# The inverse of the 16x16 blocks in two RWKV layers: rows brought to all partitions through DRAM, one product and one sum a column

## The chip, the cores and the metric

One NeuronCore of a Trainium2 chip runs the whole program in one launch. The metric is the device time of an execution in microseconds. Before the change three runs gave a median of 3160.73 us (3151.62 to 3163.76).

## What is computed

Six layers over 256 tokens of width 2048, all in float32: RWKV-7, dilated attention, pooling, a second RWKV-7 layer, then an even and an odd layer of another family. The change lies in the two RWKV layers. Their core in the reference is a recurrence over the tokens, for 32 heads of 64 channels:

```python
def step(state, inp):
    r_t, w_t, k_t, v_t, a_t, b_t = inp
    sa = jnp.einsum('bhij,bhj->bhi', state, a_t)
    state = (state * w_t[:, :, None, :] + sa[..., None] * b_t[:, :, None, :]
             + v_t[..., None] * k_t[:, :, None, :])
    y_t = jnp.einsum('bhij,bhj->bhi', state, r_t)
    return state, y_t
```

The kernel does it in chunks of 64 tokens. Within a chunk the effect of the a and b terms on each other is the inverse of a 64x64 matrix (identity minus a strictly triangular one) for each head and chunk. That inverse is built up: 16x16 diagonal blocks first, by substitution column by column; from them 32x32 blocks and then the whole by matrix products.

## The kernel before

**Projections.** `proj` (L238 on) multiplies 256 tokens by 512 columns of a weight matrix. Each 256x512 piece of weights is a DMA from SP's queue into one of three tiles `wr` (L225). ACT casts it to a high part `wh` (L220), DVE subtracts to get the low part `wl` (L221), five tiles of each, and PE makes three products for each of two token halves and each 128 rows (L262): 12 instructions of 512 columns for one `wr`. An RWKV layer has sixteen such projections (for k, r, v and a gate, `a_w_in`) and an output projection `a_w_out`, done in two passes: inputs 0 to 1535 first (`st`, L387), the last 512, which come from the layer's last two blocks, after that.

**Blocks.** `rwkv_block` treats four heads at a time, 256 channels, so there are eight blocks to a layer. A block loads its k, v, r and small weights (`ld`, `vt`, `lw`), forms factors, and multiplies them into the chunks' matrices `GM` (L842 on PE, L845 on DVE). ACT copies the 16x16 diagonal parts to `Md` (L860), and ACT and DVE select from them `Mc` (L863, L864). `Mc` is [128, 16, 8]: its partition is 16 x (one of eight 16-row groups) + row, its free axes are the column c and one of 8 units u (a head and a pair of chunks), so all 64 diagonal blocks of four heads lie in one tile. `Xc` of the same form begins as the identity. The recurrence runs over r = 0 to 14: `stream_shuffle` brings row r of each 16-row group to all partitions of the group (L871), the later columns of that row are multiplied by column r of Xc (L876), and the products are added to the columns behind it, the next one apart (L879, L881). L932 then lays Xc out as the blocks of `X`; products on PE (L929, L956) complete the inverse. Last come the four chunks in sequence (L990, L998, L1008, L1022), where each needs the state of the one before, a normalisation of the result `yt` over DVE, POOL and ACT (L1036 to L1049), and `z` (L1055), which is transposed (L277) and split for the output projection.

**Order.** The order of the code is written by a small planner: the projections advance a clock (`pump`), and blocks are generators that say with `yield` after how many microseconds they go on. A block waits there for marks of other blocks: it copies `Md` only when the block before has set `rec`, that is when its recurrence is written. `urgent` marks the blocks' instructions with a higher priority. The framework then schedules every engine's instructions by its own model of time, and each engine runs its list in that order. SP issues all loads and stores, weights among them, in one list; an instruction of it that waits holds up what stands behind.

Of the kernel before, what the change touches and what calls it, by code (L numbers as in the profile page):

```python
# [11 lines left out]
F32 = mybir.dt.float32  # L12
FR = mybir.dt.float32r
I32 = mybir.dt.int32
AF = mybir.ActivationFunctionType
OP = mybir.AluOpType
AX = mybir.AxisListType
# [97 lines left out]
class Builder:  # L115
# [562 lines left out]
    def rwkv_block(self, ia, b):  # L678

        nc, I, S = self.nc, self.I, self.S  # L680
# [9 lines left out]
        def tmp():  # L690
            return self.t("e2", B2, F32, 7)
# [112 lines left out]
        pr = tmp()  # L804
# [50 lines left out]
        Md = self.t("Md", [128, 32, 8], F32, 1)  # L855
        for i in range(4):
            rs = slice(i * 32, i * 32 + 32)
            for f in range(2):
                us = slice(f * 4, f * 4 + 4)
                nc.scalar.copy(Md[rs, :, us].rearrange("p c u -> p u c"), GM2[rs, us, (1 - i // 2) ^ f, rs])  # L860
        Mc = self.t("Mc", [128, 16, 8], F32, 1)
        odd = self.c("odd16")
        nc.scalar.activation(Mc, Md[:, 0:16], AF.Copy, scale=odd[:, 0:1])  # L863
        nc.vector.scalar_tensor_tensor(Mc, Md[:, 16:32], odd[:, 1:2], Mc, OP.mult, OP.add)  # L864
        Xc = self.t("Xc", [128, 16, 8], F32, 1)
        nc.scalar.copy(Xc, self.c("i16").unsqueeze(2).to_broadcast([128, 16, 8]))
        yield 1.0

        def shuffled(r):
            mb = self.t("mb", [128, 16, 8], F32, 3)  # L870
            nc.vector.stream_shuffle(mb[:, 0:15 - r], Mc[:, r + 1:16], [r] * 16 + [r + 16] * 16)  # L871
            return mb
        nb = shuffled(0)
        for r in range(15):
            n, mb = 15 - r, nb
            nc.vector.tensor_tensor(mb[:, 0:n], mb[:, 0:n], Xc[:, r:r + 1].to_broadcast([128, n, 8]), OP.mult)  # L876
            if r < 14:
                nb = shuffled(r + 1)
            nc.vector.tensor_tensor(Xc[:, r + 1], Xc[:, r + 1], mb[:, 0], OP.add)  # L879
            if n > 1:  # L880
                nc.vector.tensor_tensor(Xc[:, r + 2:16], Xc[:, r + 2:16], mb[:, 1:n], OP.add)  # L881
            if r % 4 == 3:
                yield 1.6
        S["rec"][b] = True
        while b > 1 and not S["chunks"][b - 2]:
            yield 1.0
# [965 lines left out]

# [9 lines left out]
```

## Time and profile before

| | us |
|---|---|
| runs, median | 3160.73 |
| profiled execution | 3169.43 |
| its span, first to last instruction | 3167.6 |
| PE busy | 3017.3 |
| DVE busy | 2247.9 |
| ACT busy | 1703.7 |
| POOL busy | 483.3 |
| mean granted clock of PE | 0.970 |

The blocks of the first RWKV layer run from about 160 to 680 us of the span, those of the second from about 1740 to 2270 us. An engine's busy time counts its instructions' durations without overlap. PE's instructions are pipelined and their ends are modelled, so that PE's busy share is an upper reading; an instruction of 512 columns is listed with some 0.39 us though the next one starts 0.23 us after it. The clock is a mean of two levels, 1.2 and 2.4 GHz, as a share of the higher.

### The profile page before, as it was taken

To read this page: it belongs to the slowest core of one execution; us is meant where nothing else is said; L and a number is where in the kernel's file an instruction comes from. 1 tells how busy PE (TensorE), PEld (TensorE's weight loads), DVE (VectorE), ACT (ScalarE), POOL (GpSimd) and SP (SyncE) were. 2 spreads that over 40 slices of the span, in tenths; PEclk is the share of its full clock that TensorE was granted. 3 is DMA by queue.
4 is the path that set the end of the run, shared out by engine and by line. 5 is a ranking of instruction groups with operands and counts; after the bars stand their busy time and mean duration, and the time that the engine had idled before them with its cause. 6 is when DMAs were issued, how large, how long until landed. Compare 5 with 4: busy or idle time off the path is not lost. (4 is left out here: it accounts for less than half of the span.)

```text
span 3167.6 us, 48383 instructions
## 1 busy us (share of the span) xinstructions
PE 3017.3 (95%) x17064; PEld 2448.3 (77%) x17064; DVE 2247.9 (71%) x4811; ACT 1703.7 (54%) x3320; POOL 483.3 (15%) x386
## 2 busy tenths in 40 slices
PE   6989999998999999999989899999999999999998
PEld 5777777777888888888867677777777788888886
DVE  7868778765667667676596787898557765756765
ACT  4555555545555555555545554545357755554554
POOL 1012223120112111010011132321201200000101
PEclk9999999998999999999999998999999999999999
DMA  7865564375556556667678555633765566665665
GB/s 235 321 209 169 176 212 148 127 232 184 178 170 179 176 173 215 192 215 214 207 263 280 200 189 175 199 121 121 246 186 157 170 186 193 182 204 169 189 185 169
DMA packets 327011, 610.77 MB, mean 193 GB/s; under 512 B 33856, under 2 KB 60776, under 8 KB 326768
## 3 DMA queue, kind: packets, MB, share of 16 engines
q1 hardware_dynamic: 326768, 607.68, 61.2%
q8 instruction: 134, 2.20, 0.3%
q14 instruction: 109, 0.89, 0.1%
HBM read 544.66 MB, written 62.93 MB: 192 GB/s over the span
## 5 line engine op out<-in xcount | busy, mean ns | idle before, releaser
L221 DVE TENSOR_TENSOR wl<-wr,wh 128x512 fp32r<-128x512 f32 x1728 | 1243.8, 731 | 713.2 <-ACT wh L220 687.3
L220 ACT CAST wh<-wr 128x512 fp32r<-128x512 f32 x1728 | 1055.6, 621 | 1078.3 <-PE qps L262 515.6
L262 PE MATMUL qps<-wl,ah 128*128 128x512 f32 x3424 | 1382.2, 404 | 7.3 <-DVE wl L221 7.2
L262 PE MATMUL qps<-wh,al 128*128 128x512 f32 x3424 | 1364.9, 399 | 2.0 <-DVE al L221 2.0
L262 PE MATMUL qps<-wh,ah 128*128 128x512 f32 x3424 | 1259.0, 404 | 46.1 <-ACT wh L220 11.8
L262 PEld LDWEIGHTS qps<-wh,ah 128*128 128x128 f32 x3424 | 655.1, 192 | 191.6 <-issue 20.4
L262 PEld LDWEIGHTS qps<-wl,ah 128*128 128x128 f32 x3424 | 657.6, 192 | 147.2 <-DVE wl L221 13.1
L262 PEld LDWEIGHTS qps<-wh,al 128*128 128x128 f32 x3424 | 656.0, 192 | 139.9 <-DVE al L221 4.5
L1107 POOL TENSOR_TENSOR q<-q,gain 128x1024 f32<-128x1024 f32 (+1 forms) x15 | 35.0, 2332 | 380.1 <-ACT sq L1101 380.1
L277 PE MATMUL qtp<-cst,q 128*128 128x128 f32 x388 | 62.4, 291 | 30.3 <-DVE q L436 9.7
L482 DVE SCALAR_TENSOR_TENSOR e<-q,vec,q 128x256 f32<-128x256 f32 x192 | 86.6, 504 | 0.0
L277 PEld LDWEIGHTS qtp<-cst,q 128*128 128x128 f32 x388 | 48.8, 149 | 43.7 <-issue 20.5
L842 PE MATMUL qtp<-q,q 64*128 64x128 f32 x512 | 76.3, 312 | 3.5 <-POOL q L815 3.3
L860 ACT COPY Md<-GM 32x128 f32<-32x128 f32 x128 | 54.8, 428 | 38.6 <-DVE GM L845 37.4
L842 PEld LDWEIGHTS qtp<-q,q 64*128 64x128 f32 x512 | 62.7, 209 | 14.6 <-issue 5.9
L1038 POOL TENSOR_TENSOR yt<-yt,gn_m 128x512 f32<-128x512 f32 x16 | 19.1, 1192 | 300.5 <-DVE gn_m L1037 191.6
L321 POOL TENSOR_TENSOR rstd<-rs_v,mhalf 128x2 f32<-128x2 f32 x7 | 5.0, 710 | 383.8 <-DVE rs_v L319 333.6
L304 POOL TENSOR_TENSOR rk_y<-ss,mhalf 128x8 f32<-128x8 f32 x16 | 28.1, 1756 | 217.7 <-DVE ss L715 117.3
L876 DVE TENSOR_TENSOR mb<-mb,Xc 128x120 f32<-128x120 f32 (+14 forms) x240 | 59.8, 249 | 0.4
L845 DVE TENSOR_TENSOR GM<-qtp,cst 128x512 f32<-128x512 f32 x64 | 43.0, 684 | 18.7 <-PE qtp L842 16.7
L871 DVE STREAM_SHUFFLE mb<-Mc 128x120 f32<-128x120 f32 (+14 forms) x240 | 50.6, 223 | 0.1
L881 DVE TENSOR_TENSOR Xc<-Xc,mb 128x112 f32<-128x112 f32 (+6 forms) x224 | 47.6, 213 | 0.1
(377 smaller groups left out, 3032.6 us busy)
## 6 DMA issues: line engine op xcount, KB each, us to landing
wr<-a_w_in SPq DMA_DIRECT2D x256, 512.0 KB
wr<-b_w_in SPq DMA_DIRECT2D x160, 512.0 KB
wr<-odd_w_in SPq DMA_DIRECT2D x128, 512.0 KB
wr<-even_w_in SPq DMA_DIRECT2D x72, 512.0 KB
wr<-a_w_out SPq DMA_DIRECT2D x64, 512.0 KB
wr<-c_w_in SPq DMA_DIRECT2D x64, 512.0 KB
ah<-mix SPq DMA_DIRECT2D x32, 512.0 KB
al<-mix SPq DMA_DIRECT2D x32, 512.0 KB
```

The source lines that it names most:

```text
L220: self.nc.scalar.copy(hi, src)
L221: (eng or self.nc.vector).tensor_tensor(lo, src, hi.bitcast(F32), OP.subtract)
L262: nc.tensor.matmul(o[:, cs], u[:, kk, sl], v[k][:, cs], start=st and x == 0 and c1 == 0, stop=sp and x == 2, skip_group_check=True)
L277: nc.tensor.transpose(q[:, f, t * 128:t * 128 + 128], src[:, t, (fp * 2 + f) * 128:(fp * 2 + f) * 128 + 128], self.ident)
L482: ins = nc.vector.scalar_tensor_tensor(m[:, f], st.xx[c][:, ft], mu, st.h[c][:, ft], OP.mult, OP.add)
L842: nc.tensor.matmul(qs[hp][:, c], BK[rs, f, c], AR[rs, f, c], start=True, stop=True)
L845: nc.vector.tensor_tensor(GM[:, f * 2 + hp].rearrange("p (q a) n -> p q (a n)", a=2), qs[hp].rearrange("p (q a) n -> p q (a n)", a=2), gma ...
L860: nc.scalar.copy(Md[rs, :, us].rearrange("p c u -> p u c"), GM2[rs, us, (1 - i // 2) ^ f, rs])
L871: nc.vector.stream_shuffle(mb[:, 0:15 - r], Mc[:, r + 1:16], [r] * 16 + [r + 16] * 16)
L876: nc.vector.tensor_tensor(mb[:, 0:n], mb[:, 0:n], Xc[:, r:r + 1].to_broadcast([128, n, 8]), OP.mult)
L881: nc.vector.tensor_tensor(Xc[:, r + 2:16], Xc[:, r + 2:16], mb[:, 1:n], OP.add)
L1107: nc.gpsimd.tensor_tensor(e3, e3, gain.unsqueeze(1).to_broadcast([128, 2 * nh, 128]), OP.mult)
```

## The change

`Mc` now gets the identity added in the first of its two instructions, which thereby moves from ACT to DVE. `Mc` is stored to DRAM (`md`, one for each block) and read back eight times by SP, once for each 16-row group, so that each of the group's 16 partitions holds all 16 rows: `MB` is [128, 16 rows, 16 columns, 8 units], 8 KB on each partition. Column c of the inverse is then the product of column c of the rows 0 to c with the columns 0 to c of Xc, and a sum over the rows. The `yield`s in between are other ones: 5 after the loads and 1 after each four columns. The last line of the diff takes the memory that is reserved for descriptors of dynamic DMA down to 1024 bytes.

```diff
-        nc.scalar.activation(Mc, Md[:, 0:16], AF.Copy, scale=odd[:, 0:1])
+        nc.vector.scalar_tensor_tensor(Mc, Md[:, 0:16], odd[:, 0:1], self.c("i16").unsqueeze(2).to_broadcast([128, 16, 8]),
+                                       OP.mult, OP.add)
         nc.vector.scalar_tensor_tensor(Mc, Md[:, 16:32], odd[:, 1:2], Mc, OP.mult, OP.add)
+        md = self.dram.tile([128, 128], F32, name="md%d_%d" % (ia, b))
+        nc.sync.dma_start(md, Mc.rearrange("p c u -> p (c u)"))
+        MB = self.t("MB", [128, 16, 16, 8], F32, 1)
+        for i in range(8):
+            blk = md[i * 16:i * 16 + 16, :]
+            nc.sync.dma_start(MB[i * 16:i * 16 + 16].rearrange("p r c u -> p (r c u)"),
+                              bass.AP(tensor=blk.tensor, offset=blk.offset, ap=[[0, 16], [1, 2048]]))
         Xc = self.t("Xc", [128, 16, 8], F32, 1)
         nc.scalar.copy(Xc, self.c("i16").unsqueeze(2).to_broadcast([128, 16, 8]))
-        yield 1.0
-
-        def shuffled(r):
...
-        nb = shuffled(0)
-        for r in range(15):
-            n, mb = 15 - r, nb
-            nc.vector.tensor_tensor(mb[:, 0:n], mb[:, 0:n], Xc[:, r:r + 1].to_broadcast([128, n, 8]), OP.mult)
-            if r < 14:
-                nb = shuffled(r + 1)
-            nc.vector.tensor_tensor(Xc[:, r + 1], Xc[:, r + 1], mb[:, 0], OP.add)
-            if n > 1:
-                nc.vector.tensor_tensor(Xc[:, r + 2:16], Xc[:, r + 2:16], mb[:, 1:n], OP.add)
-            if r % 4 == 3:
-                yield 1.6
+        yield 5.0
+        for c in range(1, 16):
+            pr = self.t("mb", [128, 16, 8], F32, 2)
+            nc.vector.tensor_tensor(pr[:, 0:c + 1], MB[:, 0:c + 1, c], Xc[:, 0:c + 1], OP.mult)
+            nc.vector.tensor_reduce(Xc[:, c], pr[:, 0:c + 1].rearrange("p r u -> p u r"), AX.X, OP.add)
+            if c % 4 == 3:
+                yield 1.0
         S["rec"][b] = True
...
-    nc = bacc.Bacc("TRN2", target_bir_lowering=False, num_devices=1)
+    nc = bacc.Bacc("TRN2", target_bir_lowering=False, num_devices=1, dynamic_dma_scratch_size=1024)
```

In the changed kernel L864 and L866 are the two instructions for `Mc`, L868 the store, L872 the loads, L879 the product and L880 the sum; what stands behind them has a line number one lower than before (L1022 is L1021).

Three places of the engines' lists show what moves. SP, third block of the first layer, before (`kkb`, `vt`, `lw` and `ld` are loads of blocks, `v` and `k` stores of projections, `wr` weights):

```order
L225 DMA wr<-a_w_in 128x2x512
L329 DMA kkb<-a_rows 128x256
L687 DMA vt<-v_1_138 128x2x256
L225 DMA wr<-a_w_in 128x2x512 x7
L695 DMA lw<-a_w2x 97x256
L695 DMA lw<-a_a2x 97x256
L602 DMA k_2_131<-st 128x512
```

and of the changed kernel:

```order
L329 DMA kkb<-a_rows 128x256
L225 DMA wr<-a_w_in 128x2x512
L687 DMA vt<-v_1_138 128x2x256
L225 DMA wr<-a_w_in 128x2x512 x6
L868 DMA md_2_3236<-Mc 128x128
L872 DMA MB<-md_2_3236 16x2048 x8
L695 DMA lw<-a_w2x 97x256
L602 DMA k_2_131<-st 128x512 x2
L695 DMA lw<-a_a2x 97x256
```

The store of `Mc` and the eight loads come in behind six of the weight loads, and the loads stand right behind the store that they read.

DVE, seventh block of the second layer, before, from the instruction that completes `Mc`:

```order
L864 SCALAR_TENSOR_TENSOR Mc<-Md,cst,Mc 128x128
L871 STREAM_SHUFFLE mb<-Mc 128x120
L871 STREAM_SHUFFLE mb<-Mc 128x112
L876 TENSOR_TENSOR mb<-mb,Xc 128x120
L879 TENSOR_TENSOR Xc<-Xc,mb 128x8
L881 TENSOR_TENSOR Xc<-Xc,mb 128x112
L876 TENSOR_TENSOR mb<-mb,Xc 128x112
L871 STREAM_SHUFFLE mb<-Mc 128x96
```

and of the changed kernel, from the first of the two for `Mc`:

```order
L864 SCALAR_TENSOR_TENSOR Mc<-Md,cst 128x128
L1017 TENSOR_TENSOR S<-qgy,S 128x256
L866 SCALAR_TENSOR_TENSOR Mc<-Md,cst,Mc 128x128
L221 TENSOR_TENSOR wl<-wr,wh 128x512
...
L879 TENSOR_TENSOR mb<-MB,Xc 128x16
L880 TENSOR_REDUCE Xc<-mb 128x8
L221 TENSOR_TENSOR wl<-wr,wh 128x512
L879 TENSOR_TENSOR mb<-MB,Xc 128x24
L958 COPY W<-qgm 32x8x32
L1001 COPY uv<-qgy 64x128
L880 TENSOR_REDUCE Xc<-mb 128x8
```

Three shuffles followed at once before; now eight instructions of other steps stand between `Mc` and the first product, and in the recurrence each product is followed by the sum that needs it, at once or behind other work.

PE, last block of the second layer, before, from its last L1022 on to the transposes of its `z`:

```order
L262 MATMUL qps<-wl,ah 128x512
L1022 MATMUL qgy<-uv,GM 64x64 x4
L262 MATMUL qps<-wh,al 128x512
L262 MATMUL qps<-wl,ah 128x512
...
L262 MATMUL qps<-wh,al 128x512
L277 MATMUL qtp<-cst,z 128x128 x4
L262 MATMUL qps<-wh,ah 128x512 x2
```

and of the changed kernel:

```order
L262 MATMUL qps<-wl,ah 128x512
L262 MATMUL qps<-wh,al 128x512
L1021 MATMUL qgy<-uv,GM 64x64 x4
L277 MATMUL qtp<-cst,z 128x128 x4
L262 MATMUL qps<-wh,ah 128x512
L262 MATMUL qps<-wl,ah 128x512
```

Between the block's last instruction for `y` and the transposes of its `z` stood 75 weight products, and now there are none. The weight products behind that point, 213 before in this layer, are 84.

## Rows read from the trace of the kernel before

**Rows 1.** The page's busy shares: engine, us (share) xinstructions

```profile
PE 3017.3 (95%) x17064; PEld 2448.3 (77%) x17064; DVE 2247.9 (71%) x4811; ACT 1703.7 (54%) x3320; POOL 483.3 (15%) x386
```

**Rows 2.** Table by stretches: start:end, length, busy us by engine, PE clock, DMA, GB/s

```profile
160.00:620.00 460.00, 437.34 (x3555) 346.15 (x3553) 357.43 (x1145) 246.70 (x546) 109.78 (x96) 0.95 0.53 173
1740.00:2210.00 470.00, 438.99 (x3598) 347.04 (x3596) 382.63 (x1176) 247.50 (x552) 115.55 (x97) 0.93 0.52 170
```

**Rows 3.** PE's waits, 1740 to 2210 us: who, for whom, us, times, longest

```profile
PE qtp L724 <- DMA lw<-a_a2x: 9.2, 5, 4.1
PE qtp L724 <- DVE mb L876: 2.5, 1, 2.5
...
PE qgm L929 <- DVE Y L938: 0.7, 1, 0.7
PE qgm L929 <- DVE W L943: 0.3, 1, 0.3
```

**Rows 4.** Timeline, last block: start, us, engine, line, operation, tiles

```profile
2148.58 0.35 DVE L864 SCALAR_TENSOR_TENSOR Mc<-Md,cst,Mc 128x128 f32<-128x128 f32 x1 [0.96 <-ACT Mc L863]
2149.54 0.28 DVE L876 TENSOR_TENSOR mb<-mb,Xc 128x120 f32<-128x120 f32 x1
2149.85 0.17 DVE L879 TENSOR_TENSOR Xc<-Xc,mb 128x8 f32<-128x8 f32 x1
...
2168.76 1.14 DVE L932 TENSOR_TENSOR X<-Xc,cst 128x512 f32<-128x512 f32 x1
...
2174.89 0.51 PE L929 MATMUL qgm<-Y,GM 64*64 64x64 f32 x10
```

**Rows 5.** Groups by line, DVE, 160 to 2210 us: xcount | busy, mean ns

```profile
L876 DVE TENSOR_TENSOR mb<-mb,Xc 128x120 f32<-128x120 f32 (+14 forms) x240 | 59.8, 249 | 0.4
L871 DVE STREAM_SHUFFLE mb<-Mc 128x120 f32<-128x120 f32 (+14 forms) x240 | 50.6, 223 | 0.1
L881 DVE TENSOR_TENSOR Xc<-Xc,mb 128x112 f32<-128x112 f32 (+6 forms) x224 | 47.6, 213 | 0.1
L879 DVE TENSOR_TENSOR Xc<-Xc,mb 128x8 f32<-128x8 f32 x240 | 46.2, 192 | 0.8
...
L1036 DVE TENSOR_REDUCE gn_m<-yt 128x8 f32<-128x512 f32 x14 | 9.5, 677 | 0.1
```

**Rows 6.** Timeline of DVE, seventh block of the second layer

```profile
2099.09 0.27 DVE L876 TENSOR_TENSOR mb<-mb,Xc 128x112 f32<-128x112 f32 x1
2099.28 0.26 DVE L871 STREAM_SHUFFLE mb<-Mc 128x96 f32<-128x96 f32 x1
...
2099.70 0.26 DVE L876 TENSOR_TENSOR mb<-mb,Xc 128x104 f32<-128x104 f32 x1
...
2105.50 0.21 DVE L876 TENSOR_TENSOR mb<-mb,Xc 128x48 f32<-128x48 f32 x1
...
2105.94 0.20 DVE L876 TENSOR_TENSOR mb<-mb,Xc 128x40 f32<-128x40 f32 x1
```

**Rows 7.** Timeline, odd layer: the bounce through DRAM that it has

```profile
2727.41 0.30 SPq L1658 DMA_DIRECT2D md<-gr  x1
2729.96 0.35 SPq L1692 DMA_DIRECT2D mb<-md  x1
...
2734.19 0.48 DVE L1704 SCALAR_TENSOR_TENSOR Dm<-mb,od_c,od_m 128x256 f32<-128x256 f32 x1 [4.15 <-DMA mb<-md]
```

**Rows 8.** ACT's waits for weights, 1740 to 2210 us

```profile
ACT wh L220 <- DMA wr<-a_w_in: 24.8, 12, 5.3
```

**Rows 9.** Chain that ended last, 2930 to 3004 us: start, us, what

```profile
2933.70 69.86 PE qps L262 x308
```

**Rows 10.** Timeline, end of the second RWKV layer

```profile
2255.53 0.46 PE L1022 MATMUL qgy<-uv,GM 128*64 128x64 f32 x8
...
2272.94 0.77 PE L262 MATMUL qps<-wh,ah 128*128 128x512 f32 x1 [6.44 <-DVE st L387]
...
2275.16 0.69 DVE L1055 SCALAR_TENSOR_TENSOR z<-yt,z 128x512 f32<-128x512 f32 x1 [1.17 <-POOL yt L1049]
```

More of the change, by code (lines that the diff above doesn't have):

```diff
@@ L862, in rwkv_block @@
         odd = self.c("odd16")
-        nc.scalar.activation(Mc, Md[:, 0:16], AF.Copy, scale=odd[:, 0:1])
+        nc.vector.scalar_tensor_tensor(Mc, Md[:, 0:16], odd[:, 0:1], self.c("i16").unsqueeze(2).to_broadcast([128, 16, 8]),
+                                       OP.mult, OP.add)
         nc.vector.scalar_tensor_tensor(Mc, Md[:, 16:32], odd[:, 1:2], Mc, OP.mult, OP.add)
+        md = self.dram.tile([128, 128], F32, name="md%d_%d" % (ia, b))
[5 more added lines that the diff above has]
+                              bass.AP(tensor=blk.tensor, offset=blk.offset, ap=[[0, 16], [1, 2048]]))
         Xc = self.t("Xc", [128, 16, 8], F32, 1)
         nc.scalar.copy(Xc, self.c("i16").unsqueeze(2).to_broadcast([128, 16, 8]))
-        yield 1.0
-        def shuffled(r):
-            mb = self.t("mb", [128, 16, 8], F32, 3)
-            nc.vector.stream_shuffle(mb[:, 0:15 - r], Mc[:, r + 1:16], [r] * 16 + [r + 16] * 16)
-            return mb
-        nb = shuffled(0)
-        for r in range(15):
-            n, mb = 15 - r, nb
-            nc.vector.tensor_tensor(mb[:, 0:n], mb[:, 0:n], Xc[:, r:r + 1].to_broadcast([128, n, 8]), OP.mult)
-            if r < 14:
-                nb = shuffled(r + 1)
-            nc.vector.tensor_tensor(Xc[:, r + 1], Xc[:, r + 1], mb[:, 0], OP.add)
-            if n > 1:
-                nc.vector.tensor_tensor(Xc[:, r + 2:16], Xc[:, r + 2:16], mb[:, 1:n], OP.add)
-            if r % 4 == 3:
-                yield 1.6
+        yield 5.0
[5 more added lines that the diff above has]
+                yield 1.0
         S["rec"][b] = True
```

## The prediction

> **What bounds the kernel now.** I read the page's busy shares first. The reader is to see that TensorE (PE) is busy 95% of the span and VectorE (DVE) 71% [rows 1]. The change touches the two RWKV layers alone, so next comes the table by stretches for the parts of them in which the eight blocks run, 160 to 620 us and 1740 to 2210 us [rows 2]. Two things are to be seen there. DVE is at 357.4 of 460 us and 382.6 of 470 us, and PE is still busy 437.3 and 439.0 us, at a mean clock of 0.95 and 0.93. So PE stands idle 23 and 31 us, and the lower of its two clock levels takes another 23 us (5% of 460) and 33 us (7% of 470). These 110 us are all that a relief in these stretches could ever give back.
>
> Then PE's own waits in the second stretch, by who ended them [rows 3]. DVE stands behind nine rows of 2.5 down to 0.3 us, 12.2 us together. PE hardly ever waits for what the recurrence makes: its first product after it is L929, and the two rows of L929 are 0.7 and 0.3 us. Last I looked at one block's pace, the last of the second layer [rows 4]: Mc is complete at 2148.93, the inverse's blocks are laid out by L932 from 2168.76, and PE begins L929 only at 2174.89. The recurrence is part of a path of 26 us with air in it.
>
> **The change, part by part.** *The sum is made against the profiled execution's own 3169.43 us (span 3167.6 and 1.8 around it); the runs' median, 3160.73, is 0.9973 of that, and I scale by it at the end.*
>
> *DVE.* Per block 59 instructions go (15 shuffles, 15 products, 15 short and 14 long sums), 30 come, and a second scalar_tensor_tensor for Mc. By durations the old ones are (59.8 + 50.6 + 47.6 + 46.2) / 16 = 12.8 us a block [rows 5]. But that counts overlaps twice. In a stretch where they stand back to back, one step lasts from L876 at 2099.09 to L876 at 2099.70, 0.61 us, and late in the recurrence from 2105.50 to 2105.94, 0.44 us [rows 6]. The shuffle behind the first L876 starts at 2099.28, 0.08 us before that has ended: an instruction that does not need its neighbour does so. Fifteen steps at about 0.51 make 7.6 us. The new product for column c has 8 (c+1) elements, 16 to 128; old products of 40, 48 and 112 elements take 0.20, 0.21 and 0.27 us [rows 6]. The new sum's form is not in the trace. The nearest is L1036, 677 ns for 512 elements [rows 5]; down the same line as the products (about 0.15 us and 1 ns an element) it is 0.16 to 0.28 us too. Each new instruction needs the one before. Such a pair, L876 at 2149.54 (0.28) and L879 at 2149.85, starts 0.03 us after the end [rows 4]. So 30 at a mean of 0.22 cost 30 x 0.25 = 7.5 us where they stand alone, and 30 x 0.14 = 4.2 us where other work stands between; the order of the changed kernel has about half of each. With 0.35 us for L864's twin [rows 4] that is 4.6 to 7.9 us against 7.6. DVE is given back between -0.3 and 3.0 us a block; I take the middle, 1.3, some 20 us in all. By whole durations it would be 12.8 - 6.6 - 0.35 = 5.8 us a block, 93 us in all.
>
> The Trainium skill's page "VectorE: DVE Perf Modes", section "The DRAIN you can't avoid", says that the next instruction cannot issue until the pipe of the last has emptied; it adds that one that is not held starts earlier. By its first sentence an instruction costs DVE its whole duration and the saving is the 93 us; the starts in [rows 6] speak for the second.
>
> What of it reaches the end? PE's waits for DVE are 12.2 us in the second stretch and, with less idle time in the first, at most some 9 there: 21 us in both. DVE gets 2% lighter (1.3 us of the 58 us that a block takes). I take -5 us, a quarter of these waits. The bounds are 0 (other rows fill the freed time) and -49 (all 21, and half of the 56 us of the lower clock).
>
> *ACT.* One activation a block goes. ACT is busy 247.5 of 470 us [rows 2], and its work on the weights covers it: nothing; if it were on the path it would be a fraction of a microsecond a block.
>
> *SP and DMA.* Each block adds a store of 64 KB and eight loads of 128 KB, 17 MB in all. Both stand in SP's queue among the weight loads: SP halts at the store until DVE has made Mc, and at the first load until the store has landed. In seven of the sixteen blocks the loads stand right behind the store. The kernel has one such bounce already, in the last layer [rows 7]: store at 2727.41, first load at 2729.96, so 2.55 us, and the first use of what it brings at 2734.19. An issue takes 0.35 us there, eight 2.8 us. So a block holds SP up to 5.4 us, and behind it are queued weight tiles, for which ACT and then PE wait. What covers that are three raw weight tiles and two and a half split pairs. The cover has holes: ACT already waits 24.8 us in twelve waits for weights in the second stretch [rows 8], and PE 9.2 us in five for another small load, lw [rows 3]. I take +6 us, a fifth of such a wait's 1.8 us in each block; bounds 0 and 16 x 5.4 = +86.
>
> *The recurrence's latency.* From Mc to the first product it now needs 6.8 us for the bounce (2727.41 to 2734.19), 2.8 us for the issues, about 8 us of DVE and the 1.1 us of L932: 19 of the 26 us of [rows 4]. Nothing, unless SP halts for 7 us more.
>
> *The order.* In the order of the changed kernel PE's block work stands later among the weight products. In the first layer the difference is small. In the second, behind the last L1022 of the last block, 213 of the layer's L262 are left before and 84 after; of those before, 75 stand ahead of the transposes of that block's result, and after none. One L262 lasts 69.86 / 308 = 0.227 us [rows 9], so 75 are 17 us of cover. What they covered is the chain from y to z, from the end of L1022 at 2255.99 to that of L1055 at 2275.85, 19.9 us [rows 10]. In the changed kernel PE stands still that long, or down to half of it if ACT and DVE, with no weights to split meanwhile, hand it on without queueing (an estimate). Taken off is what PE loses there before, 6.4 us at 2272.94 [rows 10], which now lies under other work. I take 18 - 6 = +12 us, bounds +3 and +22 (the whole chain and the split of the transposes behind it, nothing taken off). The 129 L262 that moved ahead (29 us of work) now lie between the block's steps, where PE stood idle 31 us in the second stretch: -4 us, bounds 0 and -15.
>
> **Sum.** 3169.4 - 5 + 6 + 12 - 4 = 3178 us, times 0.9973: 3170 us, 0.3% above before. What a measurement of this kernel can tell from no change is 0.5%, 16 us; so the forecast is no change that shows. Its own range is 3150 to 3186.
>
> **Rivals.**
> *Faster: DVE was what held PE up.* If the saving is 93 us, DVE falls from 81% to 71% of the stretch. Let half of PE's 21 us of waits for it and half of the 56 us of the lower clock go, and the new idle stretch at the end be at its lower bound: 3169.4 - 38 + 3 = 3134, scaled 3126. For it speaks that DVE is at its fullest here; against it that PE's waits name DVE so little, and the starts in [rows 6].
> *Slower: the store's landing holds the weights.* If in each block the 2.55 us between store and load reach PE, 16 x 2.55 = 41 us come on top of the +12 and -4: 3218, scaled 3210. It decides from the point at which a halt of SP outlasts the weight tiles in store. For it speaks that ACT waits for weights already and that lw made PE wait; against it that those waits of ACT hardly came through to PE, whose waits in that stretch have no row for L262, the weight products, at all.
> *Slower: the end of the second layer alone.* At its upper bound, with SP as above: 3169.4 + 22 + 6 = 3197, scaled 3189.
> *The recurrence was hidden and stays so, and the rest is nothing:* 3161, inside the forecast.
>
> **How the numbers follow.** The forecast and the hidden case together have 0.40, the faster one 0.25, the slower two 0.22 and 0.13. So faster by over 0.5% 0.25, within 0.5% 0.40, slower 0.35. The range reaches from the faster case to the first slower one, 3125 to 3212; beyond them lie the far bounds of SP (+86) and of DVE (-49), 2 in 10.
>
> **What would show it.** Right: DVE's busy time falls by 70 to 110 us while the second stretch of blocks is hardly shorter; PE shows one wait of 10 to 20 us for z near the second layer's end; L929 still waits for nothing; the loads of MB begin about 2.5 us after the store. Wrong: ACT's waits for a_w_in grow by more than 40 us (the slower rival), the clock of the two stretches rises to 0.98 or PE's waits for DVE vanish (the faster one), or L929 begins to wait for X.

## The result and the profile after

The changed kernel takes **3247.6 us** (median of 4 runs, 3246.0 to 3260.1) against 3162.1 for the kernel before on the same chip: **1.029 times, 95% interval 1.027 to 1.031**. The medians are 86 us apart (the ratio is of the means), and the time lies outside the predicted range (3125 to 3212). The profiled execution has a span of 3246.8 us. By the issue times of weight loads, the first RWKV layer ends 47 us later than before (first load of the next layer's `b_w_in` at 770.8 against 723.8), the second takes 780.2 us in place of 739.9 (from its first `a_w_in` to the first `even_w_in`), and the rest is 8 us shorter.

The page's busy line, after, stands against [rows 1]:

```profile
PE 3036.6 (94%) x17064; PEld 2456.8 (76%) x17064; DVE 2228.3 (69%) x4123; ACT 1701.5 (52%) x3304; POOL 479.6 (15%) x384
```

DVE has 688 instructions less and is busy 19.6 us less. The table by stretches, against [rows 2], for the parts in which the eight blocks now run:

```profile
160.00:660.00 500.00, 443.32 (x3477) 348.61 (x3476) 346.33 (x792) 239.87 (x530) 114.93 (x97) 0.91 0.61 176
1780.00:2290.00 510.00, 453.27 (x3579) 356.83 (x3576) 370.72 (x839) 250.34 (x548) 115.49 (x97) 0.92 0.61 177
```

The stretches are taken 40 us longer, as the blocks now run longer. PE idles 57 us in each (23 and 31 before), its mean clock is down from 0.95 and 0.93 to 0.91 and 0.92, and the DMA share is up from 0.53 to 0.61. What idles PE, second stretch, against [rows 3]:

```profile
PE qtp L724 <- DMA lw<-a_a2x: 20.8, 7, 7.5
PE qtp L738 <- DMA lw<-a_v2x: 12.4, 3, 5.1
PE qgy L1021 <- DVE S L1015: 9.8, 2, 6.7
```

and in the first:

```profile
PE qgy L1021 <- DVE S L1017: 19.8, 4, 6.1
PE qps L262 <- ACT st L601: 12.8, 2, 12.2
PE qps L262 <- DVE wl L221: 8.4, 5, 6.2
```

L928 (L929 before), PE's first product after the recurrence, has no row. PE waits for other things: small loads (lw), and results of DVE and ACT that are late without being part of the recurrence (S is the state's update, wl the second half of a split weight). Over the whole of both layers PE idles 158 us, 97 before; the waits that DVE ends rise from 39 to 76 us, those that lw ends from 10 to 33 us. What makes DVE late stands in its own timeline, last block of the second layer, against [rows 4]:

```profile
2225.14 0.35 DVE L866 SCALAR_TENSOR_TENSOR Mc<-Md,cst,Mc 128x128 f32<-128x128 f32 x1
...
2231.24 0.60 DVE L1001 COPY uv<-qgy 64x128 f32<-64x128 f32 x2
2239.92 0.17 DVE L879 TENSOR_TENSOR mb<-MB,Xc 128x16 f32<-128x16 f32 x1 [8.09 <-DMA MB<-md]
2240.13 0.17 DVE L880 TENSOR_REDUCE Xc<-mb 128x8 f32<-128x16 f32 x1
2240.33 0.18 DVE L879 TENSOR_TENSOR mb<-MB,Xc 128x24 f32<-128x24 f32 x1
...
2241.12 0.68 DVE L221 TENSOR_TENSOR wl<-wr,wh 128x512 fp32r<-128x512 f32 x1
...
2244.80 0.42 DVE L1015 TENSOR_TENSOR S<-qgy,fdb 128x256 f32<-128x256 f32 x1
```

DVE runs its list in order. The first product stands in it and waits 8.09 us for MB, and behind it stand a weight split (2241.12) and the state's update (2244.80), which need nothing of MB. SP at the same place, the bounce, against [rows 7]:

```profile
2225.51 0.34 SPq L868 DMA_DIRECT2D md<-Mc  x1
2229.64 3.57 SPq L872 DMA_DIRECT2D MB<-md  x8
2233.31 0.39 SPq L225 DMA_DIRECT2D wr<-a_w_in  x1
```

From the end of Mc (2225.49) to the first product it is 14.4 us; over the sixteen blocks the mean is 15.0 (0.1 to the store, 4.1 to the first load, 4.9 to the last load, 5.9 from there to the product). The recurrence ends 39.5 us after Mc (mean of sixteen), 24.1 before. All of DVE's idle time in front of L879, by what was last to arrive:

```profile
L879 DVE TENSOR_TENSOR mb<-MB,Xc x240: 164/232/1359, 189.0 to 2264.2; 128x16 f32<-128x16 f32 x8, 128x32 f32<-128x32 f32 x8, 128x48 f32<-128x48 f32 x8, 128x64 f32<-128x64 f32 x8
...
  DMA MB<-md: 63.7, 9
  DMA lw<-a_v2x: 24.5, 3
  DMA ld<-r: 12.8, 1
  DMA rows<-a_rows: 9.3, 1
  DMA v<-st: 6.8, 1
  DMA k<-st: 5.0, 1
```

These are 122 us in sixteen waits, one a block, 3.5 to 12.8 us long (the product reads nothing but MB and Xc; the other names are of DMAs that share a semaphore with the loads). PE idles 53 us inside these sixteen stretches: results of DVE end 21 us of that, lw 20, results of ACT and POOL 12. At the end of the second layer, against [rows 10]:

```profile
PE qtp L277 <- DVE z L1054: 12.3, 1, 12.3
```

and ACT's waits for weights, second stretch, against [rows 8]:

```profile
ACT wh L220 <- DMA wr<-a_w_in: 21.6, 8, 8.2
```

### The profile page after: what moved, and what is told of

It reads as the page before. It is cut to its first block, busy times and chain, and to the rows that moved or that the text cites. A ratio compares the mean times of both kernels' runs of the same rounds, so it can differ in the third digit from the quotient of the medians.

```text
span 3246.8 us, 47923 instructions
## 1 busy us (share of the span) xinstructions
PE 3036.6 (94%) x17064; PEld 2456.8 (76%) x17064; DVE 2228.3 (69%) x4123; ACT 1701.5 (52%) x3304; POOL 479.6 (15%) x384
## 5 line engine op out<-in xcount | busy, mean ns | idle before, releaser
L262 PE MATMUL qps<-wl,ah 128*128 128x512 f32 x3424 | 1378.4, 403 | 14.6 <-DVE wl L221 14.4
L879 DVE TENSOR_TENSOR mb<-MB,Xc 128x16 f32<-128x16 f32 (+14 forms) x240 | 68.4, 285 | 125.8 <-DMA MB<-md 63.7
L277 PEld LDWEIGHTS qtp<-cst,q 128*128 128x128 f32 x388 | 48.8, 149 | 44.0 <-issue 19.6
L880 DVE TENSOR_REDUCE Xc<-mb 128x8 f32<-128x16 f32 (+14 forms) x240 | 67.6, 281 | 3.8
L1021 PE MATMUL qgy<-uv,GM 128*64 128x64 f32 x512 | 34.8, 248 | 34.0 <-DVE S L1017 21.0
L1021 PEld LDWEIGHTS qgy<-uv,GM 128*64 128x64 f32 x512 | 24.2, 147 | 50.6 <-DVE S L1017 22.5
```

The source lines that it names most:

```text
L262: nc.tensor.matmul(o[:, cs], u[:, kk, sl], v[k][:, cs], start=st and x == 0 and c1 == 0, stop=sp and x == 2, skip_group_check=True)
L277: nc.tensor.transpose(q[:, f, t * 128:t * 128 + 128], src[:, t, (fp * 2 + f) * 128:(fp * 2 + f) * 128 + 128], self.ident)
L879: nc.vector.tensor_tensor(pr[:, 0:c + 1], MB[:, 0:c + 1, c], Xc[:, 0:c + 1], OP.mult)
L880: nc.vector.tensor_reduce(Xc[:, c], pr[:, 0:c + 1].rearrange("p r u -> p u r"), AX.X, OP.add)
L1021: nc.tensor.matmul(gy[kr[f], hh], GM[:, hh, c, to[f]:to[f] + 64], UV[:, hh * 64:hh * 64 + 64], start=first, stop=True, skip_group_check=True)
```

## The experiments

All were run with the kernel before beside them on the same chip; ratios are to it, with 95% intervals. Where a sum takes two of them, it is in us of 3160. The runs are called e1 to e18.

**The bounce without anyone waiting for it, in the changed kernel and in the kernel before.** First the products read Mc in place of MB; store and loads stay.

```diff
-            nc.vector.tensor_tensor(pr[:, 0:c + 1], MB[:, 0:c + 1, c], Xc[:, 0:c + 1], OP.mult)
+            nc.vector.tensor_tensor(pr[:, 0:c + 1], Mc[:, 0:c + 1], Xc[:, 0:c + 1], OP.mult)
```

> The changed kernel, but the products of the recurrence read Mc where they read MB, so nobody waits for the eight loads; the store, the loads and SP's halts stay (the inverse is not computed from the right rows). Theory 1, the first product waits for MB at the head of DVE's queue and everything behind it on DVE waits too (122 us of idle DVE in the changed kernel): 3150 to 3185 us, and DVE's idle time before L879 under 10 us. Theory 2, SP's halts and 17 MB more of traffic delay the weights and the small weights lw: 3215 us or more. Theory 3, the new PE order with its uncovered end of the second layer: about 3235, if the end stays uncovered (here 72 weight products cover it again, so at most 15 us less than the changed kernel).

Measured (e1): 3195.8, 1.011 (1.010 to 1.013), between the two ranges. The recurrence ends 24.1 us after Mc, as before. Then the other way round: the kernel before, its shuffles and products untouched, with the store and the eight loads put ahead of Xc.

```diff
+        md = self.dram.tile([128, 128], F32, name="md%d_%d" % (ia, b))
+        nc.sync.dma_start(md, Mc.rearrange("p c u -> p (c u)"))
+        MB = self.t("MB", [128, 16, 16, 8], F32, 1)
+        for i in range(8): ...
         Xc = self.t("Xc", [128, 16, 8], F32, 1)
```

> The kernel before with its 59 instructions, plus the store of Mc and the eight loads, which nobody reads. Theory 1: 3160 to 3190 us, since no DVE instruction waits for the loads. Theory 2: 3215 to 3250 us, most of the loss, with PE's waits for lw and ACT's waits for weights as in the changed kernel (33 us and 70 us).

Measured (e2): 3211.1, 1.016 (1.014 to 1.018), again between the ranges. So the bounce alone, read by no one, costs 36 us in the one and 51 in the other, and what comes with the wait for MB is 1.029 - 1.011, some 55 us. Not all of that is the wait: at the end of the second layer e1 has 72 weight products again between the last product for y and the transposes of z, and PE waits 3 us there in place of 13, so some 10 us belong to the order.

**The new form without DRAM.** The rows are spread by sixteen shuffles on DVE; product and sum stay as in the changed kernel.

```diff
-        nc.sync.dma_start(md, Mc.rearrange("p c u -> p (c u)"))
-        for i in range(8): ...
+        def spread(r):
+            nc.vector.stream_shuffle(MB[:, r, max(r, 1):16], Mc[:, max(r, 1):16], [r] * 16 + [r + 16] * 16)
```

> The changed kernel's form of the recurrence (one product, one sum a column), but with its rows put on the partitions by sixteen shuffles on DVE, so no store, no loads, no halt of SP and no wait of DVE. If the two waits are the loss, only the later end of the layer (+12) and some DVE work (16 x 0.25 = 4 us a block more than in the changed kernel, 64 us in all, beside a PE that is the bound) are left: 3160 to 3185. If the new form itself, or where it puts the block's work among the weight products, costs: 3200 to 3240.

Measured (e7): 3149.3, 0.996 (0.994 to 0.998). It is faster than the kernel before, by 11 us, and below what I expected. So neither the new form nor the smaller memory for descriptors, which e7 keeps, costs anything that shows; the whole loss of the changed kernel, some 100 us between these two (1.029 - 0.996), lies in the bounce and in what goes with it in the order (other `yield`s, and the end of the second layer, which has 72 weight products there in e7). That the 11 us come from a cheaper recurrence isn't shown: DVE's busy time is 2258.7 us, 11 more than before.

**One load in place of eight.**

```diff
-        for i in range(8): ...
+        nc.sync.dma_start(MB.rearrange("p r c u -> p (r c u)"),
+                          bass.AP(tensor=md.tensor, offset=md.offset, ap=[[2048, 8], [0, 16], [1, 2048]]))
```

> The changed kernel with one load of 1 MB in place of eight of 128 KB: SP issues one instruction instead of eight (4.9 us from the first issue to the last go). Theory 1: the first product comes some 4 us earlier, DVE's wait falls from 7.6 to 3 or 4 us a block, 3205 to 3225 us; if the one load is slower in landing, less. Theory 2: the traffic is the same, SP's halt is the same but for the issues: 3225 to 3245 us.

Measured (e3): 3294.6, 1.043 (1.041 to 1.045): 45 to 47 us slower still, against both expectations. From the issue to the first product it is 14.3 us on the mean (10.8 with eight), and DVE's waits grow from 122 to 181 us. The Trainium skill, page "DMA: Bandwidth & Descriptors", section "Rules for kernel authors", says that an outermost dimension below 16 confines a DMA to at most that many of the 16 engines; the source here has 8. The trace agrees in kind: the loads' 8 KB packets, the only ones of that size in their queue, overlap to at most 10 or 11 at a time in e3 and to 16 or 17 with eight loads. The pair e9 and e18 below shows the same counts.

**The order: recurrence later.** The first product is tied behind a weight split five pieces later (e4); then (e8) the store, the loads and the product are each put some pieces later.

```diff
-        yield 5.0
+        while self.wcount < w0 + 5 and tries < 40: ...
+                self.tc.add_manual_dep(ins.ins, self.last_wl.ins.name, ORDER, reason="product behind weight splits")
```

> The changed kernel, but the recurrence is written five weight pieces later and its first product is ordered behind the last weight split written by then: 55 DVE instructions stand between Mc and the first product on the mean, not 10. Loads, SP's list and the uncovered end of the second layer stay. Theory 1: DVE's idle time before L879 falls from 122 to under 30 us, 3165 to 3200 us. Theory 2 and theory 3: 3225 us or more.

Measured (e4): 3252.5, 1.030 (1.028 to 1.032). DVE's idle time at the first products falls to 18.6 us, and nothing is won, as theories 2 and 3 had it. But the run changes more than the wait: the recurrence ends 63 us after Mc (39.5 in the changed kernel); MB has one buffer, so the next block's loads come only when the late recurrence has read it (up to 39 us behind their store); and the end of the first layer is now bare too (PE waits 12.4 us for z).

```diff
+        yield from later(2)
+        ins = nc.sync.dma_start(md, Mc.rearrange("p c u -> p (c u)"))
+        yield from later(2)
...
+        yield from later(3)
```

> The changed kernel, with its order alone moved: the store stands two weight pieces later in SP's queue, the loads two pieces behind the store, and the first product behind the split of a piece three later, so that each finds its data there (a piece is used up in about 2.7 us). Same traffic, same instructions. If the halts of SP and the wait of DVE are the loss, 3160 to 3190, with SP's waits for Mc and md under 20 us (73 before) and DVE's in front of the first products under 30 us (122). If traffic or the recurrence's own work is it, 3210 to 3250.

Measured (e8): 3241.9, 1.025 (1.023 to 1.028). DVE waits 0.7 us in front of the first products, but the recurrence ends 66 us after Mc, SP still stands 90 us at store and loads (99 in the changed kernel), and both layers now end bare (PE waits 12.3 and 11.6 us for z). The largest rows of SP's waits at the loads (L880), store (L874), in e8:

```profile
SPq L880 <- DMA wr<-a_w_in: 31.0, 14, 4.4
SPq L880 <- DMA md<-Mc: 14.7, 6, 5.9
SPq L874 <- DVE Mc L866: 13.5, 4, 7.6
```

My expectation of under 20 us failed at the first of them: a load waits for earlier DMAs that have no data for it (see e18). So the wait was traded against lateness, with little change of the time.

**The store and the loads from POOL's queue.**

```diff
-        nc.sync.dma_start(md, Mc.rearrange("p c u -> p (c u)"))
+        nc.gpsimd.dma_start(md, Mc.rearrange("p c u -> p (c u)"))
```

(and the loads likewise)

> The changed kernel, with the store and the eight loads issued from POOL's queue instead of SP's. POOL is busy 15% and then halts where SP did. If SP's halts and DVE's wait for MB both cost, SP's part (37 to 52 us) goes and DVE's stays: 3195 to 3215. If the traffic is the first part: 3240 to 3255. If POOL's own work (rk_y, kk, yt) is held up by the halts or the loads land later from there, it is above 3255.

Measured (e6): 3250.6, 1.028 (1.026 to 1.030), where the reading by traffic had put it. SP no longer halts, POOL does, 115 us for Mc and 48 for md; the recurrence ends 46.7 us after Mc, while DVE stands only 21 us at the first products. The expectation that SP's part would go failed, and as in e4 and e8 less standing of DVE won nothing.

**Bytes without halts.** The kernel before with eight loads from a weight tensor in place of md, and no store.

```diff
+            blk = self.I["a_w_in"][ia, 0][i:i + 1, :]
+            nc.sync.dma_start(MB[i * 16:i * 16 + 16]..., bass.AP(tensor=blk.tensor, ..., ap=[[0, 16], [1, 2048]]))
```

> The kernel before, with eight loads of 128 KB a block into a tile that nobody reads; they read a piece of the weight tensor instead of a stored Mc, and there is no store. So SP issues the same 128 loads, and 16 MB move, but SP waits neither for Mc nor for a landing. If SP's halts are what cost 52 us in the kernel with the whole unread bounce (3211), most of that goes: 3160 to 3178. If the traffic and the issues (128 x 0.42 = 54 us of SP's time) are it, it stays at 3200 to 3215.

Measured (e5): 3225.1, 1.020 (1.016 to 1.023), but not what I meant to measure: with nothing to wait for, the second layer's 64 loads were issued between 1243 and 1352 us, inside other layers. e9 ties each load behind the weight load that stands there:

```diff
+            self.tc.add_manual_dep(ins.ins, self.last_wd.ins.name, ORDER, reason="loads behind weight loads")
```

> The kernel before with eight unread loads of 128 KB a block from the weight tensor, no store; this time each block's loads are tied behind the weight load that stands there, so that they are issued in the two RWKV layers, among the weights, as in the changed kernel (without the tie the second layer's loads had been issued two layers early, 1250 to 1350 us, and the first layer's in one go). The bytes and the issues are there, no wait for Mc and none for a landing store. If the bytes in front of the weights are what cost 52 us in the kernel with the whole unread bounce: 3195 to 3215. If the halts: 3160 to 3175.

Measured (e9): 3180.7, 1.005 (1.003 to 1.007): +16 to 18 us, between the ranges. **Halts without bytes:** store and eight loads of 1 KB.

```diff
+            nc.sync.dma_start(MB[i * 16:i * 16 + 16],
+                              bass.AP(tensor=blk.tensor, offset=blk.offset, ap=[[0, 16], [1, 16]]))
```

> The counterpart: the kernel before with the store of Mc and eight unread loads a block that wait for it, but each brings 1 KB (16 partitions of 64 bytes) in place of 128 KB. SP's issues and its halts for Mc and for the store are those of the changed kernel, the bytes are gone. If the bytes cost: 3160 to 3172. If the halts: 3195 to 3215. In between, both do.

Measured (e10): 3164.4, 1.0005 (0.999 to 1.002): nothing that shows, with SP standing 94 us at store (L866) and loads (L870), of which the largest rows:

```profile
SPq L870 <- DMA md<-Mc: 36.6, 15, 6.2
SPq L866 <- DVE mb L878: 35.7, 10, 8.2
```

Apart, bytes cost 16 to 18 us and halts 0 to 5; together (e2) they cost 51.

**DVE's wait without the bytes.** The version with shuffles, plus the store and one load of 4 KB, which the first product needs.

```diff
+        nc.sync.dma_start(md, Mc.rearrange("p c u -> p (c u)"))
+        nc.sync.dma_start(MB[:, 0, 1], bass.AP(tensor=md.tensor, offset=md.offset + 8, ap=[[2048, 8], [0, 16], [1, 8]]))
```

> The version with sixteen shuffles (3149), and on top of it the store and one load of 4 KB that brings one row of one column of the same values into the spread rows, so that the first product waits for a round trip through DRAM, without the bytes. DVE then stands some 4 to 6 us before the first product of each block, 65 to 95 us in all. If DVE's wait in order costs what the changed kernel seemed to show (changed kernel against the one whose products don't read MB: 52 us for 122 us of wait), this is 3149 + 28 to 41 = 3177 to 3190, and more with SP's halts. If DVE has the room and only bytes cost: 3149 to 3162.

Measured (e11): 3177.4, 1.005 (1.003 to 1.007), 28 us above e7. DVE's idle time in front of the products (L881) in e11:

```profile
  DMA MB<-md: 47.0, 12
```

So 47 us of wait, less than expected, and 28 us at the end. Halts alone cost next to nothing in e10, so most of this comes with the wait for the load. It isn't the standing of DVE alone: the first `yield` is 5 here and 1 in e7, and the recurrence ends 31.3 us after Mc (27.4 in e7).

**Four raw weight tiles in place of three,** to see whether the halts merely outlast the tiles in store: in the kernel with the unread bounce (e12), the kernel before (e13), the shuffled version (e14) and the changed kernel (e15).

```diff
-        raw = self.t("wr", shape, F32, 3)
+        raw = self.t("wr", shape, F32, 4)
```

> The kernel before with the whole unread bounce (3211 with three raw weight tiles), and four raw weight tiles in place of three, in all layers. If halts and bytes cost only together because their sum (some 6.8 us of halts, 3.4 of issues and the time of 1 MB) outlasts the three tiles (8 us), one more tile of 2.7 us takes half of the loss: 25 us or less above the kernel before with four tiles. If the lost time is the DMA's own, or comes from other small tensors (lw, st) that are held up as well, 40 to 55 us stay.

> The control: the kernel before with four raw weight tiles and nothing else. ACT's waits for weights shrink; PE hardly waited for them: 3145 to 3162 under every theory.

> The version with sixteen shuffles (3149) and four raw weight tiles: 3135 to 3150. A candidate to beat both kernels; no theory of the loss hangs on it.

> The changed kernel with four raw weight tiles. DVE's wait for MB and the bare end of the second layer are as they were (some 35 and 15 us); the part of halts and bytes (46 to 50 us) should halve if it is a matter of how many tiles are in store: 3215 to 3230. If it isn't, 3235 to 3250.

Measured: e12 3169.9, 1.002 (1.001 to 1.004); e13 3114.2, 0.985 (0.982 to 0.987); e14 **3093.8, 0.977 (0.976 to 0.979)**; e15 3220.7, 1.017 (1.015 to 1.019). The fourth tile is worth 47 us by itself, far more than I expected of it, but the bounce costs no less on top of it: 56 us from e13 to e12 (51 with three tiles), 107 from e13 to e15 (86). So my theory of the three tiles fell; e15 lies in the range that I had given for it only because its control, e13, fell by 47 as well. What is later with four tiles are small tensors of the next block. DVE's wait for k in e12,

```profile
DVE kk L710 <- DMA ld<-k: 34.7, 6, 10.5
```

and in e13:

```profile
DVE kk L710 <- DMA ld<-k: 8.1, 4, 4.1
```

e14 beats both kernels, and its stretches stand against [rows 2]: PE at 0.98 and 0.97 of the clock, idle 16 and 22 us.

```profile
160.00:620.00 460.00, 443.63 (x3675) 350.84 (x3675) 383.49 (x1088) 256.98 (x563) 119.56 (x101) 0.98 0.55 179
1740.00:2210.00 470.00, 447.85 (x3696) 352.42 (x3692) 393.12 (x1062) 250.46 (x549) 126.26 (x103) 0.97 0.55 178
```

**Each part doubled.** A second small store and load behind the tiny bounce, and sixteen loads of 128 KB in place of eight.

```diff
+        nc.sync.dma_start(md2, MB)
+        nc.sync.dma_start(MB2, md2)
```

> The kernel before with the tiny unread bounce (3164, so 2 us lost with 94 us of halts of SP), and behind it in each block a second store of the 8 KB just loaded and a load that waits for it: three more round trips' worth of halts (the load's landing, the store's landing), some 6 to 8 us more a block, hardly a byte. If what is behind SP has a slack that halts use up first and then reach PE: 40 us or more above before. If halts without bytes never reach PE: under 12 us.

```diff
-        for i in range(8):
+        for i in range(16):
```

> The kernel before with sixteen unread loads of 128 KB a block in place of eight (3181), none of which waits for a store: 34 MB in all, no wait for Mc. If each byte costs the same time: 3160 + 2 x 18 = 3196, up to 3202. If the slack is used up by bytes as well as by halts, the second eight cost more than the first: 3205 to 3230.

Measured: e16 3181.6, 1.007 (1.004 to 1.010), between its ranges; e17 3234.7, 1.022 (1.017 to 1.026), above both. Halts: 94 us cost 2, 132 us cost 21. Bytes: 16 MB cost 18, 34 MB 69 to 73. Both grow faster than in proportion. That is in keeping with a slack that is used up, and so with parts that don't add up, but no run shows the slack itself.

**The same bytes in one load.**

```diff
-        for i in range(8):
-            ins = nc.sync.dma_start(MB[i * 16:i * 16 + 16]...
+        ins = nc.sync.dma_start(MB..., bass.AP(tensor=blk.tensor, ..., ap=[[2048, 8], [0, 16], [1, 2048]]))
```

> The kernel before with one unread load of 1 MB a block in place of the eight of 128 KB (3181), tied to the same place, no store. In the order each load waits on one of eight semaphores that all DMAs share in turn, so that it can't be issued before the DMA eight places ahead has landed; eight loads go once round, and SP waited 44 us in front of them though they depend on nothing. If these places are what bytes cost (the weights' prefetch is emptied), one load waits under 10 us and the time is 3160 to 3170. If the landing of 1 MB in front of the weights is it: 3176 to 3200, since one load lands later than eight (14.3 against 10.8 us in the earlier pair).

Measured (e18): 3208.2, 1.016 (1.014 to 1.019), 28 to 36 us above e9 and above both ranges. In front of its loads SP waits no time at all, in e9 these:

```profile
SPq L868 <- DMA wr<-a_w_in: 36.8, 18, 3.8
SPq L868 <- DMA al<-mix: 4.0, 3, 2.3
```

So the places in the queue are not what these bytes cost, and that theory falls too. That it is the time they take to land in front of the weights and the lw fits, but isn't shown: from the issue to the end of the last packet it is 11.4 us in e9 and 14.0 in e18 on the mean, and PE's wait for lw in the second layer is 25.1 us in e9, and in e18:

```profile
PE qtp L724 <- DMA lw<-a_a2x: 31.0, 6, 8.2
PE qtp L738 <- DMA lw<-a_v2x: 4.7, 1, 4.7
```

## Why the prediction was wrong

The loss falls into three parts, each the difference of two runs: new form -12 (e7 against before; -11 by the medians), the unread bounce +48 (e1 against e7), and what comes with the wait for MB +55 (the changed kernel against e1), some 10 of it at the bare end of the second layer. They add up to the 91 us of the ratio by construction. A second measure of the middle part is e2, +51; e1 against the kernel before gives +36. Two terms of mine failed, by about as much: the recurrence's latency, put at nothing, and SP and DMA, put at +6. My terms:

*DVE, -5.* The relief came out as taken, 19.6 us of DVE's busy time for some 20, though not each price did: products and sums take 0.28 us on the mean, priced 0.22, so that the agreement is in part luck. The 70 to 110 us that I gave as the sign of being right did not fit this term and was wrong. No part of the relief is to be seen at the end, where DVE idles 122 us more at its first products; e1, where nobody waits, ends the recurrence 24.1 us after Mc, no sooner than before.

*SP and DMA, +6.* Mis-sized: 36 to 51 us. I priced only the halt and let the weight tiles in store cover it. Halts alone are covered indeed (e10, +2). I set no price on the 16 MB themselves, which land in front of the weights and of lw (e9, +16 to 18, and 51 with the halts). The slower rival, 41 us from the store's landing, had about the size, but not the cause, and its sign (ACT's waits for weights up by more than 40 us) didn't come: 48.1 in the first stretch (32.1 before, over a shorter one), 21.6 in the second (24.8).

*The recurrence's latency, "Nothing, unless SP halts for 7 us more".* **This is the step that failed.** I asked whether PE waits for the recurrence, and it doesn't: L928 has no row of waits. But in my 19 us the recurrence stood with 8 us of DVE's bare time, and I held that against 26 us in which the old instructions are spread, among other work, over 23 us. The air in that path was not free. The new instructions are spread just as wide, 24.5 us from the first product to the end (24.1 from Mc in e1), so that the bounce came on top almost whole: 15.4 us a block. And it is longer than I wrote, 15.0 us from Mc to the first product for my 9.6, because the loads stand among weight loads. Nor did I ask what stands behind the first product in DVE's own list. There the bounce is 122 us in which DVE does nothing, with weight splits and state updates behind it, and 53 us of PE's idle time lie in these stretches. All this is some 45 us, the 55 less the end of the layer.

How much of the 45 is DVE's standing and how much that the block runs later, the runs don't separate. In e11, 47 us of standing go with 28 us at the end, but there the recurrence is later too. In e4, e6 and e8 DVE stands 19, 21 and 1 us, the recurrence ends 63, 47 and 66 us after Mc, and the time is about the same; the waits of PE that DVE ends are 85, 86 and 78 us there, no fewer than the changed kernel's 76. In e4 and e8 one more bare end, some 10 us, is in the time. So the time is not set by the standing alone.

*The order, +12 at the end of the layer.* Right in kind: PE waits 12.3 us for z there, within the predicted 10 to 20, where it waited 6.4 [rows 10]. The term was net of that 6.4, so what came is +6, half of it and within its bounds. The -4 for the products that moved ahead can't be seen under the rest.

The two slower cases had 0.35, and the result lies above them both, in the 2 in 10 beyond the range.

## What to carry to other kernels

Before a wait is called hidden, write down what is queued behind the waiting instruction on its own engine, and hold latencies against each other with the same work spread between their steps; that the consumer on the critical engine doesn't wait says nothing about it. Here a round trip through DRAM on the queue that feeds the weights cost by bytes and by halts together, and more than the sum of both (51 us against 18 and 2). The version with shuffles on DVE itself, though it has more instructions than the changed kernel, was some 100 us faster; and one more weight tile was worth 47 us, four times what that version won over the kernel before.

## What the runs showed that I had not expected

- One load of 1 MB with eight outer rows takes longer to land than eight of 128 KB (14.3 against 10.8 us to the first use) and costs more even if no one reads it (e18 against e9, 28 to 36 us).
- SP stands in front of independent loads: 44 us in e9, 103 us in e17, for DMAs that have nothing to do with them (the DMA eight places ahead in the order, whose semaphore they share).
- The page's busy time hardly tells of any of this: PE 3004 to 3037 us and DVE 2224 to 2259 us in the kernel before, the changed kernel, e1, e2 and e7, whose times lie between 3149 and 3248.
